# Attention scores of two query blocks written together, with their two causal masks as neighbours on TensorE

## Chip, core and metric

The kernel runs on one core of one Trainium2 chip. The metric is device time in microseconds, the median of several executions. One further execution is recorded by the hardware profiler; all rows below come from that one.

## The reference

A trunk of two layers for 1024 tokens of width 1024: a state-space layer, then keys, values and forget gates computed once, then an attention layer with 16 heads of 64. The change lies in the attention alone:

```python
s = jnp.einsum('bhqd,bhkd->bhqk', qi, kt)
s = s + fqi[..., None] - fk[:, :, None, :]
qpos = i * Q_BLOCK + jnp.arange(Q_BLOCK)
s = jnp.where(kpos[None, :] <= qpos[:, None], s, -jnp.inf)
p = jax.nn.softmax(s, axis=-1)
return jnp.einsum('bhqk,bhkd->bhqd', p, vt)
```

A block is 128 queries; block i sees the keys 0 to 128 (i + 1). Everything is float32.

## The kernel before

The state-space layer, the output of that layer and the tokens' keys, values and queries come first and fill the first 820 us. Float32 matmuls are split into parts that are exact in the chip's 4-byte matmul format, so that a product is two or three matmuls into one PSUM buffer.

The attention runs over 64 steps, `steps`: for each of 16 heads the four pairs of query blocks c = 0 to 3 (blocks 2c and 2c + 1, so 128 and 256 keys for c = 0, up to 896 and 1024 keys for c = 3). The loop at L1140 does `ahead` for the step two further on, which calls `scores`, then `values` for the present step, then some matmuls of another product as filling (`zb`, the gate projection, later `f`, the output projection).

`scores(hd, c)` treats the two blocks of a step one after the other. Up to 512 keys are one piece, more are two. A piece is a PSUM buffer `sp`: two score matmuls (L1010, L1011; high and low part of the keys), and for a block's last piece a third one (L1013) with bf16 operands, the identity times a triangle of 1e30 that hides the later keys. One VectorE instruction (L1015) adds the forget term, writes the piece to `pr` and leaves the running minimum in `mx` (the signs are turned round). Then come Exp on ScalarE (L1018), a reciprocal on VectorE (L1019) and the scaling on GpSimd (L1020).

`values` transposes the scaled rows on TensorE (`tp`, L1043), copies them rounded on ScalarE (`pth`, L1045), takes what rounding lost on VectorE (`ptl`, L1046), multiplies both with the values (`ov`, L1049 and L1050) and adds the two halves of the result (`oc`, L1056, after the copy `ob`, L1052). The gate's strips end with L991 on ScalarE and L992 on VectorE.

What is shared: `sp` has three PSUM buffers (pool `psb`), `tp` three (`psa`), `ov`, `zb` and `f` two together (`pj`); `pr` has two SBUF buffers for each c. The order of the instructions on each engine is not the order of the text: a list scheduler, which works with times of its own, lays it down when the kernel is built, and each engine then runs its list in order. `tc.issue_after(x)` keeps what it encloses behind `x` on x's engine.

Of the kernel before, what the change touches and what calls it, by code (L numbers as in the profile page):

```python
# [12 lines left out]
F32 = mybir.dt.float32  # L13
F32R = mybir.dt.float32r
BF16 = mybir.dt.bfloat16
AF = mybir.ActivationFunctionType
ALU = mybir.AluOpType
# [3 lines left out]
P = 128  # L21
# [25 lines left out]
def trunk(tc, a, out):  # L47
    nc = tc.nc
    V, S, G, T, Q = nc.vector, nc.scalar, nc.gpsimd, nc.tensor, nc.sync
    top = ExitStack()  # L50
    with top:
# [24 lines left out]
        vec, at0 = {}, 0  # L76
# [105 lines left out]
        with l0:  # L182
# [89 lines left out]
            for k in range(KT):  # L272
# [3 lines left out]
                if k < 2:  # L276
                    w01[k] = weight_strip(a["a_w_in"][k], [P, KT, P])
                V.scalar_tensor_tensor(out=s_a[:, k:k + 1], in0=mod[:, 8 + k:9 + k], scalar=sc1[:, k:k + 1], in1=ga[:, k:k + 1],
                                       op0=ALU.add, op1=ALU.mult)
                for i in range(2):  # L280
                    hi, xs = act[0][k][i][:, 0:HL], xt[:, HL * i:HL * i + HL]
                    S.activation(hi, xs, AF.Copy, scale=s_a[:, k:k + 1])
                    V.scalar_tensor_tensor(out=act[1][k][i][:, 0:HL], in0=xs, scalar=s_a[:, k:k + 1], in1=hi.bitcast(F32),
                                           op0=ALU.mult, op1=ALU.subtract)
# [12 lines left out]
            for k in range(KT):  # L297
                last_mod = mod_tile(k)
                hi, b = act[0][k][1][:, HL:], vec["modb"][:, k:k + 1]
                m = mod[:, k:k + 1].broadcast_to([P, 2])  # L300
                S.activation(hi, m, AF.Identity, bias=b)
                last_lo = V.scalar_tensor_tensor(out=act[1][k][1][:, HL:], in0=m, scalar=b, in1=hi.bitcast(F32),
                                                 op0=ALU.add, op1=ALU.subtract).ins
# [407 lines left out]
            for k in range(KT):  # L711
                pool, tag = ((s5, "bb"), (s5, "bbs"), (s5, "x1m"), (s5, "x2m"), (sbm, "min_"), (s5, "ut"), (sb, "uu"), (sb, "uu"))[k]
# [21 lines left out]
        with l0b:  # L734
# [38 lines left out]
            for e, i in OUT_SEQ:  # L773
# [8 lines left out]
                if sum(seen) and n < 40:  # L782
                    with tc.issue_after(xd):
# [3 lines left out]
                                       op0=ALU.mult, op1=ALU.add)  # L787
# [26 lines left out]
        with l1a:  # L814
# [103 lines left out]
            for j, job in enumerate(("v0", "v2", "k0", "k2", "q0", "q2")):  # L918
                kind, n0 = job[0], int(job[1])
                if job == "q0":  # L920
# [11 lines left out]
                    at0 = top.enter_context(tc.tile_pool(name="at0", bufs=2, side="right", reuse_waits="tile"))  # L932
# [27 lines left out]
        at_ = top.enter_context(tc.tile_pool(name="at", bufs=2, reuse_waits="tile"))  # L960
        msk = at0.tile([P, P], BF16, name="msk", tag="msk", bufs=1)
        G.memset(msk, 0.0)
        G.affine_select(out=msk, in_=msk, compare_op=ALU.is_ge, fill=BIG, base=0, pattern=[[-1, P]], channel_multiplier=1)
        idb = at0.tile([P, P], BF16, name="idb", tag="idb", bufs=1)
# [29 lines left out]

        def scores(hd, c):
            kk, qs, vhl, fb = hd
            prs = []
            for qi in range(2):
                i = 2 * c + qi
                nk = P * (i + 1)  # L1000
                qsl = qs[:, P * i:P * i + P]
                pr = (at0 if c < 2 else at_).tile([P, 256 * c + 256], F32, name="pr", tag=f"pr{c}")
                mx = None
                cut = nk if nk <= 512 else max(nk - 512, 512) if nk != 640 else 384
                for lo, hi in ((0, cut), (cut, nk))[:2 if nk > 512 else 1]:
                    w_ = hi - lo
                    wm_ = max(w_, 256)
                    last = hi == nk
                    sp = psb.tile([P, 512], F32, name="sp", tag="psb")
                    T.matmul(sp[:, 0:wm_], qsl, kk[:, 0, lo:lo + wm_], start=True, stop=False)  # L1010
                    T.matmul(sp[:, 0:wm_], qsl, kk[:, 1, lo:lo + wm_], start=False, stop=not last)  # L1011
                    if last:
                        T.matmul(sp[:, w_ - P:w_], idb, msk, start=False, stop=True)  # L1013
                    m0, mx = mx, at0.tile([P, 1], F32, name="mx", tag="mx", bufs=8)
                    V.tensor_tensor_reduce(out=pr[:, lo:hi], in0=sp[:, 0:w_], in1=fb[:, lo:hi], scale=1.0,  # L1015
                                           scalar=3e38 if m0 is None else m0, op0=ALU.add, op1=ALU.min, accum_out=mx)
                sm = at0.tile([P, 1], F32, name="sm", tag="sm", bufs=8)
                S.activation(pr[:, 0:nk], pr[:, 0:nk], AF.Exp, scale=-1.0, bias=mx, accum_out=sm)  # L1018
                V.reciprocal(out=sm, in_=sm)  # L1019
                G.tensor_scalar(out=pr[:, 0:nk], in0=pr[:, 0:nk], scalar1=sm, scalar2=0.0,  # L1020
                                op0=ALU.mult, op1=ALU.add)
                prs.append(pr)
            return prs

        def values(n, hd, c, prs):
# [39 lines left out]
        def ahead(j):  # L1065
            n, c = steps[j]
            for m in (n, n + 1):
                if m < NH and m not in hds:
                    hds[m] = head(m)
            return scores(hds[n], c)  # L1070
# [146 lines left out]
```

## Time and profile before

| | |
|---|---|
| median of 3 runs (lowest, highest) | 1225.78 us (1220.67, 1227.47) |
| the profiled execution: its time, its span | 1223.69 us, 1221.9 us |
| TensorE, weight loads, VectorE, ScalarE, GpSimd busy | 95%, 83%, 69%, 50%, 30% of the span |
| first and last causal mask | 820.7 us, 1121.5 us |
| masks, score matmuls, reductions | 128, 384, 192 |

The span is the time from the first to the last instruction of the profiled execution. A matmul's row gives a start and a length that includes its way through the array, so neighbours overlap; what one costs is read from the distance between the ends (start plus length) of two neighbours. A figure in brackets at a row's end is idle time of the engine before it, with what ended it. "PE" is TensorE, "PEld" its loading of weights, "DVE" VectorE, "ACT" ScalarE, "POOL" GpSimd.

### The profile page before, as it was taken

To read this page: it belongs to the slowest core of one execution; us is meant where nothing else is said; L and a number is where in the kernel's file an instruction comes from. 1 tells how busy PE (TensorE), PEld (TensorE's weight loads), DVE (VectorE), ACT (ScalarE), POOL (GpSimd) and SP (SyncE) were. 2 spreads that over 40 slices of the span, in tenths; PEclk is the share of its full clock that TensorE was granted. 3 is DMA by queue.
4 is the path that set the end of the run, shared out by engine and by line. 5 is a ranking of instruction groups with operands and counts; after the bars stand their busy time and mean duration, and the time that the engine had idled before them with its cause. 6 is when DMAs were issued, how large, how long until landed. Compare 5 with 4: busy or idle time off the path is not lost.

```text
span 1221.9 us, 20599 instructions
## 1 busy us (share of the span) xinstructions
PE 1162.0 (95%) x7542; PEld 1017.3 (83%) x7542; DVE 848.9 (69%) x1724; ACT 605.1 (50%) x1138; POOL 367.8 (30%) x568
## 2 busy tenths in 40 slices
PE   8989898997899998899989999999999999999898
PEld 6778887887778876799989989998888888888686
DVE  7889899874498767746444664448787778887421
ACT  6565766665335324322213452227677777886310
POOL 4000000000000033600133463447576666764100
PEclk9999999998989999999999999999999999999999
DMA  9754666584974885247543277518796968871242
GB/s 352 220 173 117 171 169 164 154 233 126 334 249 129 281 312 167 90 154 233 200 148 139 83 214 152 156 70 182 132 188 124 171 122 155 156 138 27 94 165 78
DMA packets 113333, 205.30 MB, mean 168 GB/s; under 512 B 17072, under 2 KB 58160, under 8 KB 111696
## 3 DMA queue, kind: packets, MB, share of 16 engines
q1 hardware_dynamic: 86272, 161.44, 41.4%
q0 software_dynamic: 24960, 37.75, 18.1%
q10 hardware_dynamic: 2000, 4.79, 1.7%
q8 instruction: 60, 0.98, 0.3%
q14 instruction: 41, 0.34, 0.1%
HBM read 146.47 MB, written 46.20 MB: 158 GB/s over the span
## 4 chain that ended last, share of the span: by engine, by line
PE 57%; DVE 16%; DMA 12%; ACT 5%; issue 5%; SPq 2%; POOL 2%; ACTq 0%; POOLq 0%; DVEq 0%
PE tkps L851 16%; PE zb L112 7%; PE pj_f L112 5%; PE tp L1043 5%; DMA modw<-modw 4%; PE u L264 4%; PE ov L1049 3%; PE ov L1050 3%; PE sp L1010 3%; DMA v_d<-vt 3%; PE sp L1011 3%; PE pj_g L112 2%; DMA mwx<-modw 2%; PE f L112 2%; DVE w_lo L101 1%
## 5 line engine op out<-in xcount | busy, mean ns | idle before, releaser
L851 PE MATMUL tkps<-wvh,aH 128*128 128x256 f32 (+1 forms) x768 | 220.5, 287 | 7.3 <-DVE vt L863 4.0
L851 PE MATMUL tkps<-wvh,aL 128*128 128x256 f32 (+1 forms) x768 | 217.1, 283 | 1.4 <-DVE aL L167 1.4
L851 PE MATMUL tkps<-wvl,aH 128*128 128x256 f32 (+1 forms) x768 | 216.7, 282 | 0.0
L851 PEld LDWEIGHTS tkps<-wvh,aH 128*128 128x128 f32 x768 | 145.2, 189 | 9.8 <-DVE vt L863 4.9
L851 PEld LDWEIGHTS tkps<-wvh,aL 128*128 128x128 f32 x768 | 145.1, 189 | 2.1 <-DVE aL L167 1.8
L851 PEld LDWEIGHTS tkps<-wvl,aH 128*128 128x128 f32 x768 | 145.3, 189 | 0.3 <-issue 0.2
L1045 ACT ACTIVATE pth<-tp 128x512 fp32r<-128x512 f32 (+1 forms) x192 | 87.2, 489 | 61.4 <-PE ov L1049 34.7
L1018 ACT ACTIVATE pr<-pr,mx 128x128 f32<-128x128 f32 (+7 forms) x128 | 98.9, 773 | 22.4 <-DVE mx L1015 21.8
L1020 POOL TENSOR_SCALAR pr<-pr,sm 128x128 f32<-128x128 f32 (+7 forms) x128 | 96.2, 761 | 40.6 <-DVE sm L1019 40.5
L1046 DVE TENSOR_TENSOR ptl<-tp,pth 128x512 fp32r<-128x512 f32 (+1 forms) x192 | 101.3, 551 | 9.0 <-ACT pth L1045 8.6
L93 ACT ACTIVATE w_hi<-w_raw 128x1024 fp32r<-128x1024 f32 x49 | 51.6, 1053 | 86.4 <-PE pj_f L112 29.5
L1015 DVE CUSTOM_DVE_ANT_0 pr<-sp,fb 128x512 f32<-128x512 f32 (+3 forms) x128 | 72.8, 569 | 21.3 <-PE tp L1043 19.9
L1049 PE MATMUL ov<-pth,vhl 128*128 128x256 f32 x320 | 85.6, 299 | 0.1
L1043 PE MATMUL tp<-ident,pr 128*128 128x128 f32 x576 | 82.9, 273 | 0.0
L874 ACT ACTIVATE hsq<-tkps 128x256 f32<-128x256 f32 x64 | 24.6, 384 | 117.8 <-PE tkps L851 112.5
L132 DVE CUSTOM_DVE_ANT_0 modw<-modw,c_b 128x1024 f32<-128x1024 f32 x48 | 58.6, 1223 | 34.0 <-DMA modw<-modw 33.7
L1050 PE MATMUL ov<-ptl,vhl 128*128 128x256 f32 x320 | 81.0, 286 | 0.2 <-DVE ptl L1046 0.2
L1010 PE MATMUL sp<-kk,qs 128*128 128x256 f32 (+2 forms) x192 | 74.5, 388 | 2.2 <-DVE mx L1015 1.9
L1043 PEld LDWEIGHTS tp<-ident,pr 128*128 128x128 f32 x576 | 65.3, 140 | 7.1 <-POOL pr L1020 0.5
L794 POOL TENSOR_TENSOR sq<-sq,sq 128x512 f32<-128x512 f32 x12 | 19.0, 1585 | 173.3 <-ACT sq L790 173.3
L877 POOL TENSOR_TENSOR hms<-hms,nhalf 128x4 f32<-128x4 f32 x64 | 67.6, 1057 | 5.0
L876 POOL TENSOR_SCALAR hms<-hms 128x4 f32<-128x4 f32 x64 | 15.2, 237 | 176.3 <-DVE hms L875 172.4
(325 smaller groups left out, 3305.4 us busy)
## 6 DMA issues: line engine op xcount, KB each, us to landing
modw<-modw SPq DMA_DIRECT2D x48, 512.0 KB, 5.1
kk<-k_d POOLq DMA_DIRECT2D x32, 512.0 KB, 6.8
wvr<-kvq_w SPq DMA_DIRECT2D x12, 1024.0 KB, 5.5
mwx<-modw SPq DMA_DIRECT2D x16, 512.0 KB, 7.5
w_raw<-a_w_in SPq DMA_DIRECT2D x16, 512.0 KB, 5.2
v_d<-vt SPq DMA_DIRECT2D x32, 256.0 KB, 2.5
fb<-f_d SPq DMA_DIRECT2D x16, 512.0 KB, 8.9
vhl<-v_d POOLq DMA_DIRECT2D x16, 512.0 KB, 9.7
```

The costliest lines, as they stand in the source:

```text
L112: T.matmul(ps, w[wt][:, k, :], act[at][k][half], start=(k == k0 and n == 0), stop=(k == k1 and n == 2))
L851: T.matmul(ps[:, 0:nv], at, wt[:, k, 0:nv], start=(n == 0), stop=(n == 3 * KT - 1))
L877: G.tensor_tensor(out=ms, in0=ms, in1=nhalf, op=ALU.pow)
L1010: T.matmul(sp[:, 0:wm_], qsl, kk[:, 0, lo:lo + wm_], start=True, stop=False)
L1015: V.tensor_tensor_reduce(out=pr[:, lo:hi], in0=sp[:, 0:w_], in1=fb[:, lo:hi], scale=1.0, scalar=3e38 if m0 is None else m0, op0=ALU.add, o ...
L1018: S.activation(pr[:, 0:nk], pr[:, 0:nk], AF.Exp, scale=-1.0, bias=mx, accum_out=sm)
L1020: G.tensor_scalar(out=pr[:, 0:nk], in0=pr[:, 0:nk], scalar1=sm, scalar2=0.0, op0=ALU.mult, op1=ALU.add)
L1043: T.transpose(out=tp[:, b, :], in_=prs[qi][:, P * (b0 + b):P * (b0 + b) + P], identity=ident)
L1045: S.activation(pth[:, 0:m, dst], tp[:, 0:m, :], AF.Copy)
L1046: V.tensor_tensor(out=ptl[:, 0:m, dst], in0=tp[:, 0:m, :], in1=pth[:, 0:m, dst].bitcast(F32), op=ALU.subtract)
L1049: T.matmul(ov, vhl[:, b, :], pth[:, b - b0, :], start=(b == 0), stop=False)
L1050: end = T.matmul(ov, vhl[:, b, :], ptl[:, b - b0, :], start=False, stop=(b == nb - 1)).ins
```

## The change

`scores` now runs over the pieces and not over the blocks: first the first pieces of both blocks where there are two, with their reductions, then the last pieces of both, four score matmuls, then the two masks directly one behind the other, then the two reductions. The mask of the second block is held behind the mask of the first, and that one behind the last score matmul, by `issue_after`. Exp, reciprocal and scaling of both blocks follow. Both `pr` buffers of a step are taken at its beginning. The instructions are the same in number and shape.

```diff
-            for qi in range(2):
-                i = 2 * c + qi
-                nk = P * (i + 1)
...
-                for lo, hi in ((0, cut), (cut, nk))[:2 if nk > 512 else 1]:
...
-                    sp = psb.tile([P, 512], F32, name="sp", tag="psb")
-                    T.matmul(sp[:, 0:wm_], qsl, kk[:, 0, lo:lo + wm_], start=True, stop=False)
-                    T.matmul(sp[:, 0:wm_], qsl, kk[:, 1, lo:lo + wm_], start=False, stop=not last)
-                    if last:
-                        T.matmul(sp[:, w_ - P:w_], idb, msk, start=False, stop=True)
-                    m0, mx = mx, at0.tile([P, 1], F32, name="mx", tag="mx", bufs=8)
...
+            for last in (False, True):
+                for qi in range(2):
+                    nk, cut = cut_of(qi)
+                    lo, hi = (cut if nk > 512 else 0, nk) if last else (0, cut if nk > 512 else 0)
+                    if hi == lo:
+                        continue
...
+                    sp = psb.tile([P, 512], F32, name="sp", tag="psb")
                     T.matmul(sp[:, 0:wm_], qsl, kk[:, 0, lo:lo + wm_], start=True, stop=False)
+                    m = T.matmul(sp[:, 0:wm_], qsl, kk[:, 1, lo:lo + wm_], start=False, stop=not last).ins
+                    work.append((qi, lo, hi, sp))
+                if last:
+
+                    for qi, lo, hi, sp in work:
+                        with tc.issue_after(m):
+                            m = T.matmul(sp[:, hi - lo - P:hi - lo], idb, msk, start=False, stop=True).ins
+                for qi, lo, hi, sp in work:
+                    pr = prs[qi]
+                    m0, mxs[qi] = mxs[qi], at0.tile([P, 1], F32, name="mx", tag="mx", bufs=8)
+                    V.tensor_tensor_reduce(out=pr[:, lo:hi], in0=sp[:, 0:hi - lo], in1=fb[:, lo:hi], scale=1.0,
+                                           scalar=3e38 if m0 is None else m0, op0=ALU.add, op1=ALU.min, accum_out=mxs[qi])
```

With other rows to place, the scheduler lays down another order from the first scores on. In TensorE's list before, 61 masks stand ahead of a transpose and 67 ahead of another matmul; in the list after, the 64 pairs stand 21 times ahead of a transpose and 43 times ahead of another matmul. One place recurs in every second head: the step with 384 and 512 keys (c = 1) of an even head. On TensorE before, from the three transposes behind a strip of the gate projection on:

```order
L1043 MATMUL tp<-ident,pr 128x128 x3
L1010 MATMUL sp<-kk,qs 128x384
L1011 MATMUL sp<-kk,qs 128x384
L1013 LDWEIGHTS idb
L1013 MATMUL sp<-msk,idb 128x128
L1010 MATMUL sp<-kk,qs 128x512
L1011 MATMUL sp<-kk,qs 128x512
L1013 LDWEIGHTS idb
L1013 MATMUL sp<-msk,idb 128x128
L1043 MATMUL tp<-ident,pr 128x128 x4
```

The same place on TensorE after:

```order
L1053 MATMUL tp<-ident,pr 128x128 x3
L1012 MATMUL sp<-kk,qs 128x384
L1013 MATMUL sp<-kk,qs 128x384
L1053 MATMUL tp<-ident,pr 128x128 x8
L1012 MATMUL sp<-kk,qs 128x512
L1013 MATMUL sp<-kk,qs 128x512
L1019 LDWEIGHTS idb
L1019 MATMUL sp<-msk,idb 128x128
L1019 LDWEIGHTS idb
L1019 MATMUL sp<-msk,idb 128x128
```

Eight transposes moved ahead of the second block's matmuls, and the first block's mask moved behind them.

On VectorE the reductions of these two blocks (384 and 512 keys), the gate, and the subtractions for the next value matmuls stand in this order before (the buffers' numbers tell the rows apart):

```order
L1015 ISA pr_10135,mx_10140<-sp_10136,fb_9759 128x384
L1015 ISA mx_10140 128x1
L1015 ISA pr_10146,mx_10151<-sp_10147,fb_9759 128x512
L1015 ISA mx_10151 128x1
L992 SCALAR_TENSOR_TENSOR o_t3_8253<-o_t3_8253,zb3_1_9677 128x512
L1046 TENSOR_TENSOR ptl_10018<-tp_10021,pth_10017 128x3x128
L1019 RECIPROCAL sm_10142<-sm_10142 128x1
L1046 TENSOR_TENSOR ptl_10018<-tp_10027,pth_10017 128x4x128
L1019 RECIPROCAL sm_10153<-sm_10153 128x1
L1046 TENSOR_TENSOR ptl_10086<-tp_10087,pth_10085 128x4x128
L1056 TENSOR_TENSOR oc_9673<-ov_9948,ob_9966 64x256
```

And after:

```order
L1023 ISA pr_10135,mx_10145<-sp_10137,fb_9759 128x384
L1023 ISA mx_10145 128x1
L1023 ISA pr_10136,mx_10147<-sp_10140,fb_9759 128x512
L1023 ISA mx_10147 128x1
L992 SCALAR_TENSOR_TENSOR o_t3_8253<-o_t3_8253,zb3_1_9677 128x512
L1056 TENSOR_TENSOR ptl_10018<-tp_10021,pth_10017 128x3x128
L1056 TENSOR_TENSOR ptl_10018<-tp_10027,pth_10017 128x4x128
L1030 RECIPROCAL sm_10149<-sm_10149 128x1
L1056 TENSOR_TENSOR ptl_10086<-tp_10087,pth_10085 128x4x128
L1066 TENSOR_TENSOR oc_9673<-ov_9948,ob_9966 64x256
```

VectorE's list hardly moved there: one reciprocal went behind the sum of the halves. What moved is the mask that its first row waits for.

## Rows read from the trace of the kernel before

**Rows 1.** The page's busy line; busy time, clock, DMA of one stretch.

```profile
PE 1162.0 (95%) x7542; PEld 1017.3 (83%) x7542; DVE 848.9 (69%) x1724; ACT 605.1 (50%) x1138; POOL 367.8 (30%) x568
...
820.00:1127.00 307.00, 304.50 (x2027) 260.20 (x2027) 250.65 (x785) 225.46 (x532) 196.09 (x342) 1.00 0.74 139
```

**Rows 2.** Who waited for whom: us in total, times, longest; TensorE, 820 to 1130.

```profile
PE sp L1010 <- DVE mx L1015: 1.9, 5, 0.7
```

**Rows 3.** The masks' line: weight loads and idle time before them (us, times).

```profile
L1013 PEld LDWEIGHTS <-idb x128: 95/96/98, 820.7 to 1121.5; 128*128 128x128 bf16 x128
...
  issue: 13.7, 64
```

**Rows 4.** Timeline of TensorE around two masks: start, length, instruction.

```profile
903.29 0.39 PE L1011 MATMUL sp<-kk,qs 128*128 128x512 f32 x1
903.52 0.23 PE L1013 MATMUL sp<-msk,idb 128*128 128x128 bf16 x1
903.56 0.36 PE L1010 MATMUL sp<-kk,qs 128*128 128x256 f32 x1
903.76 0.28 PE L1011 MATMUL sp<-kk,qs 128*128 128x256 f32 x1
903.88 0.23 PE L1013 MATMUL sp<-msk,idb 128*128 128x128 bf16 x1
903.94 0.94 PE L1043 MATMUL tp<-ident,pr 128*128 128x128 f32 x7
```

**Rows 5.** The weight loads at the first of these masks.

```profile
903.06 0.19 PEld L1011 LDWEIGHTS sp<-kk,qs 128*128 128x128 f32 x1
903.51 0.10 PEld L1013 LDWEIGHTS <-idb 128*128 128x128 bf16 x1 [0.26 <-issue]
```

**Rows 6.** TensorE at the recurring place, 927.8 to 934.3.

```profile
927.80 0.49 PE L1043 MATMUL tp<-ident,pr 128*128 128x128 f32 x3
...
928.30 0.33 PE L1011 MATMUL sp<-kk,qs 128*128 128x384 f32 x1
928.48 0.23 PE L1013 MATMUL sp<-msk,idb 128*128 128x128 bf16 x1
...
933.07 0.93 PE L1043 MATMUL tp<-ident,pr 128*128 128x128 f32 x7
934.01 0.39 PE L1049 MATMUL ov<-pth,vhl 128*128 128x256 f32 x1
```

**Rows 7.** VectorE at the same place, and two rows shortly before.

```profile
924.63 0.69 DVE L1046 TENSOR_TENSOR ptl<-tp,pth 128x512 fp32r<-128x512 f32 x1
925.24 0.74 DVE L1015 CUSTOM_DVE_ANT_0 pr<-sp,fb,mx 128x512 f32<-128x512 f32 x1
...
928.75 0.56 DVE L1015 CUSTOM_DVE_ANT_0 pr<-sp,fb 128x384 f32<-128x384 f32 x1
...
929.78 0.69 DVE L1015 CUSTOM_DVE_ANT_0 pr<-sp,fb 128x512 f32<-128x512 f32 x1 [0.47 <-PE tp L1043]
...
930.40 0.68 DVE L992 SCALAR_TENSOR_TENSOR o_t<-o_t,zb 128x512 f32<-128x512 f32 x1
931.00 0.55 DVE L1046 TENSOR_TENSOR ptl<-tp,pth 128x384 fp32r<-128x384 f32 x1
931.47 0.15 DVE L1019 RECIPROCAL sm<-sm 128x1 f32<-128x1 f32 x1
...
932.80 0.69 DVE L1046 TENSOR_TENSOR ptl<-tp,pth 128x512 fp32r<-128x512 f32 x1 [0.33 <-ACT pth L1045]
933.53 0.43 DVE L1056 TENSOR_TENSOR oc<-ov,ob 64x256 f32<-64x256 f32 x1
```

**Rows 8.** Who waited for the sum of the halves (us, times), 820 to 1127.

```profile
  PEld ov L1049: 1.8, 7
```

**Rows 9.** What ended TensorE's idle time before scores; one such wait.

```profile
  DVE mx L1015: 4.3, 10
...
1064.46 0.41 PE L1010 MATMUL sp<-kk,qs 128*128 128x384 f32 x1 [0.68 <-DVE mx L1015]
```

More of the change, by code (lines that the diff above doesn't have):

```diff
@@ L996, in scores, with cut_of @@
             kk, qs, vhl, fb = hd
-            prs = []
-            for qi in range(2):
-                i = 2 * c + qi
-                nk = P * (i + 1)
[L1001 to L1004, printed above, removed]
-                for lo, hi in ((0, cut), (cut, nk))[:2 if nk > 512 else 1]:
-                    w_ = hi - lo
-                    wm_ = max(w_, 256)
-                    last = hi == nk
+            def cut_of(qi):
+                nk = P * (2 * c + qi + 1)
+                return nk, nk if nk <= 512 else max(nk - 512, 512) if nk != 640 else 384
@@ new lines, in scores @@
+            prs = [(at0 if c < 2 else at_).tile([P, 256 * c + 256], F32, name="pr", tag=f"pr{c}") for _ in range(2)]
+            mxs, work = [None] * 2, []
+            for last in (False, True):
[4 more added lines that the diff above has]
+                        continue
+                    wm_ = max(hi - lo, 256)
+                    qsl = qs[:, P * (2 * c + qi):P * (2 * c + qi) + P]
@@ L1009, in scores @@
                     sp = psb.tile([P, 512], F32, name="sp", tag="psb")
                     T.matmul(sp[:, 0:wm_], qsl, kk[:, 0, lo:lo + wm_], start=True, stop=False)
-                    T.matmul(sp[:, 0:wm_], qsl, kk[:, 1, lo:lo + wm_], start=False, stop=not last)
-                    if last:
-                        T.matmul(sp[:, w_ - P:w_], idb, msk, start=False, stop=True)
-                    m0, mx = mx, at0.tile([P, 1], F32, name="mx", tag="mx", bufs=8)
-                    V.tensor_tensor_reduce(out=pr[:, lo:hi], in0=sp[:, 0:w_], in1=fb[:, lo:hi], scale=1.0,
-                                           scalar=3e38 if m0 is None else m0, op0=ALU.add, op1=ALU.min, accum_out=mx)
+                    m = T.matmul(sp[:, 0:wm_], qsl, kk[:, 1, lo:lo + wm_], start=False, stop=not last).ins
@@ L1017, in scores @@
+                work = []
+            for qi in range(2):
+                pr, nk = prs[qi], P * (2 * c + qi + 1)
                 sm = at0.tile([P, 1], F32, name="sm", tag="sm", bufs=8)
-                S.activation(pr[:, 0:nk], pr[:, 0:nk], AF.Exp, scale=-1.0, bias=mx, accum_out=sm)
+                S.activation(pr[:, 0:nk], pr[:, 0:nk], AF.Exp, scale=-1.0, bias=mxs[qi], accum_out=sm)
                 V.reciprocal(out=sm, in_=sm)
@@ L1021, in scores @@
                                 op0=ALU.mult, op1=ALU.add)
-                prs.append(pr)
             return prs
```

## The prediction

> **What bounds the kernel now.** I read the page's busy line first, then the table by stretches, then who waits for whom in the attention stretch, and only then single instructions. The change touches nothing before 820 us and nothing after the last causal mask at 1121.5 us, so the stretch 820 to 1127 us is all that can move. In it TensorE has an instruction under way for 304.5 of 307 us at a granted clock of 1.00, VectorE for 250.7 and ScalarE for 225.5 [rows 1]. TensorE's waits that the profile names for its matmuls of the scores are 1.9 us in five places [rows 2]. So TensorE sets the pace, and the other engines decide only at a few places where their chains are late. The sum below is therefore a sum over TensorE's stream, and after it comes a look at those places.
>
> **What a mask costs.** The 128 mask matmuls are the only ones with bf16 operands; all their neighbours are 4-byte. The unit that loads weights stood idle for 13.7 us in 64 places just before the masks' loads and was waiting for nothing that the profile shows [rows 3]. One of these: the weights of the last score matmul were loaded from 903.06, and the mask's load begins only at 903.51, when that matmul's columns have gone through, although the unit was free for 0.26 us [rows 5]. So a mask's load is not drawn ahead over its 4-byte neighbour. The price is read from ends of matmuls [rows 4]. The score matmul before the mask ends at 903.29 + 0.39 = 903.68 and the mask at 903.52 + 0.23 = 903.75: the mask costs 0.07 us itself. The matmul behind it, 256 columns wide, ends at 903.92, 0.17 after the mask, whereas the next of the same width takes 0.12 (904.04). So 0.05 us more is lost on the way out. Where transposes follow, nothing is lost on the way out: the mask at 903.88 ends at 904.11, the seven transposes at 904.88, which is 0.11 each, their usual spacing.
>
> **The change, part by part.** No instruction is added or taken away: 384 score matmuls, 128 masks, 192 reductions, the same Exp, reciprocals and scalings.
>
> (1) *Neighbours.* In TensorE's order before, 61 of 128 masks are followed by a transpose and 67 by a matmul that pays the way out. In the order after, all masks stand in 64 pairs; a pair is followed 21 times by a transpose and 43 times by a matmul that pays. So the scheduler had already covered 61 ways out with transposes, and what goes is not 64 of them but 67 - 43 = 24. At 0.05 us each that is 1.2 us less.
>
> (2) *The second mask of a pair.* No row shows a mask behind a mask. I take 0.07 us, the price of a first mask, because its own 128 columns and load are the same; then this part is zero. The lower end is 0.04 us, the shortest step from a mask's start to the next matmul's start (903.52 to 903.56) [rows 4]: 64 x 0.03 = 1.9 us less. The upper end is a mask with a full way out, 0.12 us: 64 x 0.05 = 3.2 us more. Both ends stay for the range. The Trainium skill, "TensorE: Matmul & The Clock Gate", section "Back-to-back issue gap", gives about 81 ns per matmul for a sustained run of loads and matmuls of 128 columns; worked out from that figure, an estimate, a second mask would cost 0.01 us more than I take, 0.7 us over 64 pairs, which speaks against the change. No row here shows it, and the 0.07 us of the first mask lies below it.
>
> (3) *Reductions come later, at a place where VectorE is the late one.* A pair's two masks now follow both blocks' pieces, so the first block's reduction begins later. In most places nobody cares: the transposes of a block follow its mask by 11 us and more of TensorE's stream in both orders, apart from the first seven steps. It matters once in every two heads, where the step with 384 and 512 keys meets a strip of the gate projection (or, in the last, of the output projection). Before: three transposes begin at 927.80, the first block's matmuls end at 928.63 and its mask at 928.71 [rows 6]; VectorE starts that reduction at 928.75, and between its operations up to 933.5 it idles 0.47 and 0.33 us [rows 7]. The chain ends with the sum of the two halves of the output, 933.53 + 0.43 = 933.96, which frees a PSUM buffer, and TensorE's next value matmul starts at 934.01, late: its transposes had begun at 933.07 [rows 6]. Seven such waits make 1.8 us [rows 8]. After: from 927.80 TensorE has three transposes (to 928.29), the 384-wide pair of matmuls (0.34), eight transposes (8 x 0.11), the 512-wide pair (2 x 0.23), and then the mask (0.07), which ends at 930.04; the reduction starts at 930.08. Behind it VectorE now works without a break: 0.56 and 0.62 for the two reductions, 0.60 for the gate, 0.47 and 0.61 for two subtractions, 0.15 for a reciprocal, 0.73 for the third subtraction and what lies behind it [rows 7], together 3.74. The sum of the halves starts at 933.82 and not at 933.53, and TensorE goes on 0.3 us later. ScalarE, which had the Exp of the second block ahead of the third subtraction's input, now has it behind, so it is not the later one. This sequence stands at six places in the order after: 6 x 0.3 = 1.8 us more. The ends are 0 (if the gate's operation finds its input later and slips behind) and 0.6 us per place (if ScalarE is late by one more Exp), 0 to 3.6 us.
>
> (4) *Three score buffers, two of them held.* Pieces of scores share three PSUM buffers. A pair now holds two until both masks are done. TensorE's waits for a buffer, 4.3 us in ten places with those that other instructions end, lie in the first ten microseconds and around 1063 us, where VectorE also splits the gated outputs (0.68 us at 1064.46) [rows 9]. At the beginning the new order asks for a buffer after 0.5 to 1.2 us of TensorE's stream where it was 0.9 to 1.5, while a reduction of 384 keys keeps VectorE 0.56 us and the next one behind it 0.62 [rows 7]; around 1063 us a 384-wide second piece is reduced later than before, with two splits behind it. I put down 0.8 us more for both together, half of one reduction in three places; the ends are 0 and 2 us.
>
> **The sum**: -1.2 + 0 + 1.8 + 0.8 = +1.4 us. The profiled execution took 1223.69 us (span 1221.9), which would become 1225.1; it lies 2.1 us below the median of the runs, 1225.78, and on that the sum gives 1227.2. The three runs lie 6.8 us apart, so neither is the better base, and I take the middle, **1226.2 us**. The ends add up to -1.2 - 1.9 = -3.1 (1222.7) and -1.2 + 3.2 + 3.6 + 2.0 = +7.6 (1233.4). About 0.5%, 6.1 us, is what a measurement of this kernel can tell from no change.
>
> **Rivals.**
> *The masks flow.* The second mask costs 0.04 us and VectorE's chain gives nothing back: -1.2 - 1.9 = -3.1, 1222.7 us. For it: weights and operands of both masks have one type. Against it: VectorE has no idle time left in the chain of part 3, and even this is below what can be told from no change.
> *The buffers run out, slower.* With two of three buffers held, the ring becomes the limit in the steady part too. Counting TensorE's stream between the last matmul into a buffer and its next use at the spacings of the rows, the order before has 7 places under 1.5 us, all in the first 14 us, and the order after has 23, many of them in every second head. If VectorE is behind at the 16 new ones so that the reduction ends half a microsecond after the buffer is wanted, that is 8 us: 1225.8 - 1.2 + 8 = 1232.6 us. It decides from the point where a reduction ends later than 1.0 us behind its mask at the places with 0.95 us. For it: reductions of 0.56 and 0.62 us follow each other there. Against it: the first of the two needs 0.04 + 0.56 us behind its mask when VectorE is free [rows 6, 7], which is inside 0.95. The Trainium skill, "Trainium Kernel Development and Optimization", section "Best Practices", says that consistent bubbles can mean that PSUM ran out; in this trace the bubbles are 1.9 us by name [rows 2], so it does not yet hold here.
> *The pairs don't do what they say.* The second mask's weights wait for the first as after any change of type, and a mask costs 0.12 us in a pair too: -1.2 + 3.2 + 1.8 + 0.8 = +4.6, 1230.4 us.
>
> **How the numbers follow.** Forecast 0.65, the masks flow 0.13, the buffers run out 0.14, pairs that don't pay 0.08. Only the buffers' case reaches past +0.5% (1231.9), with a small part of the last: slower 0.14. Past -0.5% (1219.7) there is no case, only a sum of luck: faster 0.04. Same 0.82. The range takes in the first, second and fourth case, 1222 to 1231; the buffers' case is left out.
>
> **What would show it.** Right: pairs whose second mask starts about 0.07 us behind the first with a matmul ending 0.17 behind it; TensorE's value matmul at the six places late by 0.5 to 0.6 us in all, freed by the sum of the halves; score matmuls waiting for the reductions' maximum 5 to 6 us in all. Part 2 is wrong if the second mask takes 0.04 or 0.12. Part 3 is wrong if VectorE's chain there has gaps or ScalarE ends it. The whole is wrong if score matmuls wait for the maximum in every second head, or if the stretch from the first mask to the last moves by over 6 us.

## The result and the profile after

The changed kernel took 1230.53 us (median of 14 runs, 1226.2 to 1235.21) and the kernel before 1224.51 (14 runs beside them, 1220.67 to 1229.13). The ratio is 1.0048, 95% interval 1.0033 to 1.0064: about 6 us slower, just inside half a per cent. In a second series it was 1228.12 us against 1224.08, ratio 1.0034 (1.0018 to 1.0049).

The page's busy line of the changed kernel, and its table by stretches (length; busy time of TensorE, its weight loads, VectorE, ScalarE, GpSimd with counts; granted clock; DMA share; GB/s). 824.61 us is the end of the last token matmul, the last work ahead of attention:

```profile
PE 1166.3 (95%) x7542; PEld 1026.5 (83%) x7542; DVE 845.2 (69%) x1724; ACT 603.2 (49%) x1138; POOL 367.4 (30%) x568
...
824.61:829.61 5.00, 1.68 (x13) 1.16 (x10) 2.21 (x5) 1.65 (x3) 1.20 (x2) 1.00 0.07 27
829.61:834.61 5.00, 4.97 (x25) 3.97 (x24) 3.60 (x17) 2.83 (x10) 2.23 (x8) 0.66 0.85 288
834.61:1131.00 296.39, 293.79 (x1963) 255.62 (x1963) 237.93 (x756) 216.39 (x514) 191.60 (x330) 1.00 0.75 138
```

The same two stretches of the kernel before, from the end of its last token matmul at 820.22:

```profile
820.22:825.22 5.00, 3.88 (x25) 2.50 (x23) 3.57 (x13) 3.29 (x9) 2.06 (x4) 1.00 0.05 21
825.22:830.22 5.00, 4.89 (x29) 3.62 (x29) 4.85 (x19) 3.95 (x11) 2.40 (x7) 1.00 0.84 295
```

The loss is to be seen in the first rows. In the first five microseconds of attention TensorE was busy for 3.88 before and is busy for 1.68 now; in the next five it is busy all the time, but at a granted clock of 0.66. In the long rest it is as full as in [rows 1].

TensorE's waits between the last token matmul and the last mask, by what ended them (us, times, longest; of waits over 0.15 us); they answer [rows 2], where five waits for the maximum made 1.9 us:

```profile
PE trps L886 <- DVE hnt L879: 1.9, 1, 1.9
PE sp L1012 <- DVE kl L891: 1.5, 1, 1.5
PE sp L1012 <- DVE mx L1023: 1.3, 1, 1.3
PE ov L1060 <- DVE ptl L1056: 0.5, 1, 0.5
```

**A measure that the experiments share.** Ten of the thirteen traces of this study have the same instructions up to the last token matmul, and it ended anywhere from 816.5 to 824.6 us. In six of them (both of the changed kernel, not the one before) a stretch of 3.4 us between 771 and 782 us had half the clock, after waits that the others have too. This scatter is no part of the change, and 1.6 us of the 9.3 us by which the first two spans differ are that stretch. So the traces are compared over **the stretch from the end of the last token matmul to the end of the last mask**: 301.46 us before (820.22 to 1121.69), 306.37 in the changed kernel (824.61 to 1130.98), 306.36 in its second trace.

Where the +4.91 us lie is worked out matmul by matmul: the distance from the end of one to the end of the next, less the median distance for its width in the kernel before. For the masks the whole distance stands. A "way out" is what the matmul behind a mask loses; the first two rows together are called mask terms below.

| us, in the stretch | before | after | difference |
|---|---|---|---|
| masks themselves (128; after: 64 first, 64 second) | 9.3 | 8.1 | -1.2 |
| ways out behind masks | 3.7 | 1.6 | -2.1 |
| waits in the first ten microseconds | 3.1 | 4.1 | +1.0 |
| matmuls at half clock there, beyond normal | 0 | 1.9 | +1.9 |
| value matmuls behind a pair, eleven places of 0.18 | 0 | 2.0 | +2.0 |
| six places with 384 and 512 keys | 1.8 | 3.0 | +1.2 |
| steps right after the beginning, to 865 us | 0.3 | 0.9 | +0.6 |
| around 1063 us, and 1083 to 1115 | 2.9 | 3.5 | +0.6 |
| all other matmuls, some 1,750 | 0.2 | 0.8 | +0.7 |

The rounded rows add up to 4.7 of the 4.91 us. So the neighbours did what the change is named for (-1.2 and -2.1), and the loss lies mainly in three other places: the beginning, the value matmuls behind a pair, and the six places with 384 and 512 keys. The experiments took them one by one.

### The profile page after: what moved, and what is told of

The parts are those of the page before. It is cut to its first block, busy times and chain, and to the rows that moved or that the text cites. A ratio compares the mean times of both kernels' runs of the same rounds, so it can differ in the third digit from the quotient of the medians.

```text
span 1231.2 us, 20643 instructions
## 1 busy us (share of the span) xinstructions
PE 1166.3 (95%) x7542; PEld 1026.5 (83%) x7542; DVE 845.2 (69%) x1724; ACT 603.2 (49%) x1138; POOL 367.4 (30%) x568
## 5 line engine op out<-in xcount | busy, mean ns | idle before, releaser
L1056 DVE TENSOR_TENSOR ptl<-tp,pth 128x512 fp32r<-128x512 f32 (+1 forms) x192 | 98.6, 549 | 13.2 <-ACT pth L1055 12.6
L1023 DVE CUSTOM_DVE_ANT_0 pr<-sp,fb 128x512 f32<-128x512 f32 (+3 forms) x128 | 70.0, 569 | 22.9 <-PE tp L1053 14.3
L1053 PE MATMUL tp<-ident,pr 128*128 128x128 f32 x576 | 78.9, 273 | 0.0
```

Of the source, the lines that this page charges most:

```text
L1023: V.tensor_tensor_reduce(out=pr[:, lo:hi], in0=sp[:, 0:hi - lo], in1=fb[:, lo:hi], scale=1.0, scalar=3e38 if m0 is None else m0, op0=ALU.a ...
L1053: T.transpose(out=tp[:, b, :], in_=prs[qi][:, P * (b0 + b):P * (b0 + b) + P], identity=ident)
L1056: V.tensor_tensor(out=ptl[:, 0:m, dst], in0=tp[:, 0:m, :], in1=pth[:, 0:m, dst].bitcast(F32), op=ALU.subtract)
```

## The three places in the trace

**The entry.** TensorE from the last token matmuls to the first pair (start, length, instruction; in brackets the idle time and what ended it):

```profile
824.45 0.38 PE L886 MATMUL trps<-ident,hnt 128*128 128x128 f32 x2
824.59 0.37 PE L1012 MATMUL sp<-kk,qs 128*128 128x256 f32 x1
824.79 0.38 PE L886 MATMUL trps<-ident,hnt 128*128 128x128 f32 x2
824.93 0.36 PE L1013 MATMUL sp<-kk,qs 128*128 128x256 f32 x1
825.13 0.38 PE L886 MATMUL trps<-ident,hnt 128*128 128x128 f32 x2
827.38 0.44 PE L886 MATMUL trps<-ident,hnt 128*128 128x128 f32 x2 [1.86 <-DVE hnt L879]
829.27 0.39 PE L1012 MATMUL sp<-kk,qs 128*128 128x256 f32 x1 [1.45 <-DVE kl L891]
829.49 0.28 PE L1013 MATMUL sp<-kk,qs 128*128 128x256 f32 x1
829.62 0.29 PE L1019 MATMUL sp<-msk,idb 128*128 128x128 bf16 x2
829.93 0.69 PE L1012 MATMUL sp<-kk,qs 128*128 128x384 f32 x1
830.41 0.52 PE L1013 MATMUL sp<-kk,qs 128*128 128x384 f32 x1
```

The masks and the last of these transposes in the kernel before, whose last token matmul ends at 820.22:

```profile
820.74 0.23 PE L1013 MATMUL sp<-msk,idb 128*128 128x128 bf16 x1
...
821.71 0.23 PE L1013 MATMUL sp<-msk,idb 128*128 128x128 bf16 x1
...
822.93 0.23 PE L1013 MATMUL sp<-msk,idb 128*128 128x128 bf16 x1
...
823.11 0.38 PE L886 MATMUL trps<-ident,hnt 128*128 128x128 f32 x2
```

The last transposes of the queries (`trps`) write into the same pool of three PSUM buffers (`psb`) as the scores, and two of their tiles are still being filled: their last input, `hnt` (normalised queries, from VectorE), comes 2.7 us behind the last token matmul. In the kernel before this wait was filled: the first block's piece was masked, reduced and its buffer taken again, so that three masks and six score matmuls ran ahead of the last `trps`, which ended 3.3 us behind the last token matmul there and 3.2 us in the changed kernel. In the changed kernel the first piece holds the third buffer until the second is there too, and the second needs a buffer of the transposes, which comes free only with `kl` (what rounding the transposed queries lost, taken by VectorE), shortly ahead of 829.27. The first block's mask, whose matmuls end at 825.29, stands behind it. Then the clock falls: from 829.96 to 833.37 the granted clock is 0.5, and the 384-wide matmul at 830.41 takes 0.52 us, 0.33 in [rows 6]. (The one at 829.93 also holds a short wait and the way out behind the masks.)

**A value matmul behind a pair.** TensorE, and VectorE at the same time:

```profile
893.62 0.28 PE L1013 MATMUL sp<-kk,qs 128*128 128x256 f32 x1
893.74 0.28 PE L1019 MATMUL sp<-msk,idb 128*128 128x128 bf16 x2
893.93 0.39 PE L1060 MATMUL ov<-ptl,vhl 128*128 128x256 f32 x1
```

```profile
892.04 0.69 DVE L1023 CUSTOM_DVE_ANT_0 pr<-sp,fb 128x512 f32<-128x512 f32 x1 [1.08 <-PE tp L1053]
...
892.65 0.61 DVE L1023 CUSTOM_DVE_ANT_0 pr<-sp,fb,mx 128x384 f32<-128x384 f32 x1
...
893.19 0.68 DVE L1056 TENSOR_TENSOR ptl<-tp,pth 128x512 fp32r<-128x512 f32 x1
```

The two masks end 0.12 us behind the score matmul (893.90 to 894.02), but the value matmul ends at 894.32, 0.30 behind the masks, where the exit from a mask to a value matmul took 0.17 before (a mask from 886.32 for 0.23 us, the value matmul behind it from 886.36 for 0.36). It reads `ptl`, which VectorE has ready at 893.87. VectorE had waited 1.08 us with the second block's unmasked reduction (892.04) at the head of its queue, for transposes of an earlier step; the first block's masked reduction was queued behind that one and the subtraction `ptl` behind both. In the kernel before, `ptl` stood between two reductions of one block [rows 7: 924.63, then 925.24].

**The place with 384 and 512 keys**, the counterpart of [rows 6] and [rows 7], in another head (TensorE, then VectorE):

```profile
899.54 0.39 PE L1013 MATMUL sp<-kk,qs 128*128 128x512 f32 x1
899.81 0.38 PE L1012 MATMUL sp<-kk,qs 128*128 128x256 f32 x1
900.03 0.28 PE L1013 MATMUL sp<-kk,qs 128*128 128x256 f32 x1
900.41 0.50 PE L112 MATMUL zb<-aH,w_hi 128*128 128x512 f32 x1
...
901.91 0.93 PE L1053 MATMUL tp<-ident,pr 128*128 128x128 f32 x7
902.59 0.38 PE L1059 MATMUL ov<-pth,vhl 128*128 128x256 f32 x1
```

```profile
898.58 0.56 DVE L1023 CUSTOM_DVE_ANT_0 pr<-sp,fb 128x384 f32<-128x384 f32 x1 [1.20 <-PE sp L1019]
...
899.06 0.69 DVE L1023 CUSTOM_DVE_ANT_0 pr<-sp,fb 128x512 f32<-128x512 f32 x1
...
899.67 0.68 DVE L992 SCALAR_TENSOR_TENSOR o_t<-o_t,zb 128x512 f32<-128x512 f32 x1
...
902.11 0.43 DVE L1066 TENSOR_TENSOR oc<-ov,ob 64x256 f32<-64x256 f32 x1
```

VectorE's reductions are late and without a break between them, as forecast, but the operation that TensorE waits for is the gate (`o_t`, over at 900.35), which frees the PSUM buffer that the next strip's matmul at 900.41 takes: 0.36 us lost there, and 0.14 at the score matmul of 899.81, which needs a score buffer. The sum of the halves (`oc`) ends at 902.54 and the value matmul at 902.59 is on time now. So 0.50 us are lost at the place where the kernel before lost 0.29, measured by the same distances, at its value matmul (the waits of [rows 8]).

## Experiments

All ratios are to the kernel before, run beside each kernel. "Stretch" is the one defined above (301.46 before, 306.37 after). `scores_old` is the function of the kernel before, put beside the new one.

**The changed kernel again.**

> The changed kernel once more, unaltered, to have a second trace of it. In the first pair of traces TensorE's stream of the changed kernel was already 4.4 us late at the last transposes ahead of attention, where both programs have the same instructions. Theory A (the loss lies in the attention: the first pair finds too few score buffers, and one place in every two heads is 0.25 us longer) expects a ratio to the kernel before of about 1.004, a first mask that starts about 3 us later behind the last of those transposes than in the kernel before, and any lead of the part ahead of attention to vary from trace to trace. Theory B (every pair of masks costs) expects the same 1.004, but no such delay at the entry. Theory C (the 6 us are scatter of the part ahead of attention) expects a ratio within 1.002.

Ratio 1.0034 (1.0018 to 1.0049), stretch 306.36, first mask 5.1 us behind the last token matmul (0.5 before). The loss is in the attention and repeats; theory C, scatter, is out for it. The delay is 4.6 us where 3 were expected.

**The first two steps as before.**

```diff
-            return scores(hds[n], c)
+            return (scores_old if j < 2 else scores)(hds[n], c)
```

> The changed kernel, with the scores of the first two steps (two of 64) written as before: each block's pieces, its mask and its reduction in one go. Theory A: TensorE no longer stands still for 1.9 and 1.5 us in front of the first scores, no half-clock stretch follows, and the time falls by about 3 us from the changed kernel's, to a ratio of about 1.002 to the kernel before. Theory B: two of 64 pairs are nothing, at most 0.2 us less than the changed kernel, ratio 1.0045. Theory C: no difference from the changed kernel or the kernel before, all within 1.002.

Ratio 1.0007 (0.9987 to 1.0026), stretch 303.60. Two of 64 pairs cost 2.8 us of the stretch and 3.3 us of the time (1.0034 to 1.0007). First mask 0.5 us behind the last token matmul; no half clock in the stretch.

**The new order of pieces without neighbours.**

```diff
-                    m = T.matmul(sp[:, 0:wm_], qsl, kk[:, 1, lo:lo + wm_], start=False, stop=not last).ins
+                    T.matmul(sp[:, 0:wm_], qsl, kk[:, 1, lo:lo + wm_], start=False, stop=not last)
...
-                if last:
-
-                    for qi, lo, hi, sp in work:
-                        with tc.issue_after(m):
-                            m = T.matmul(sp[:, hi - lo - P:hi - lo], idb, msk, start=False, stop=True).ins
+                    if last:
+                        T.matmul(sp[:, hi - lo - P:hi - lo], idb, msk, start=False, stop=True)
```

> The changed kernel's order of pieces (first both blocks' unmasked pieces, then both masked ones, then the reductions), but each mask directly behind its own score matmuls, with no wait for the other block's. It tells the new order of the pieces from the neighbours. Theory A: the second piece does not hold the first one's mask back, so the entry is like the kernel before's; the masks pay their way out alone again (about 24 x 0.05 us = 1.2 us more than neighbours), and the place in every two heads is early again: ratio about 1.000 to 1.001. Theory B: also 1.000, since no mask has a neighbour. Rival D (the order of the pieces and of the reductions itself is what costs): ratio 1.004 as for the changed kernel.

Ratio 1.0017 (0.9998 to 1.0036), stretch 304.49, first mask on time. Both lie between theory A (1.000 to 1.001) and rival D (1.004): the stretch is 3.0 us longer than before, 0.25% of the time, with no neighbours and no delay at the entry. Rival D is right in part: the order of pieces and reductions costs by itself. The value matmuls behind a mask end 0.25 us after it at ten places here too (0.17 before).

**The first two steps and the place with 384 and 512 keys of every even head as before.**

```diff
-            return scores(hds[n], c)
+            return (scores_old if j < 2 or (c == 1 and n % 2 == 0) else scores)(hds[n], c)
```

> The changed kernel, with the scores written as before in the first two steps and in the step with 384 and 512 keys of every even head (the place where VectorE's chain frees TensorE's PSUM buffer late). Some 55 of 64 pairs stay neighbours. Theory A: both sources of the loss are gone, and what stays are second masks at 0.056 us and fewer ways out: 0.5 to 1.5 us below the kernel before, ratio 0.999 to 1.000, and some 1.5 us below the kernel with only the first two steps as before. Theory B: 55 of 64 pairs still cost, ratio 1.0038. Theory C: within 1.002, like all the others.

Ratio 0.9986 (0.9970 to 1.0003), stretch 302.13: 1.5 us below the kernel with only the first two steps as before, as expected, 0.24 us for each of six places. But the stretch is still 0.7 us longer than before's, where pairs alone should have made it shorter; the eleven places of 0.30 us are all there. The ratio alone says 1.7 us less than before, and the two don't agree: its interval ends at +0.4 us.

**All pairs kept, the last transposes of the queries in another pool.**

```diff
-                    tr = psb.tile([P, 4, P], F32, name="trps", tag="psb")
+                    pool, tag = (psa, "psa") if dst is q_d and pr0 == 6 and i == 1 else (psb, "psb")
+                    tr = pool.tile([P, 4, P], F32, name="trps", tag=tag)
```

> The changed kernel, all 64 pairs kept; only the last two groups of the queries' transposes (trps, the second half of the last strip) write into the pool of three PSUM buffers that the token tiles and the transposes of the scores use (psa), and not into the one that the scores use (psb). It tests the cause of the delay at the entry by itself. Buffer theory: the first pair finds its second buffer free, so the first mask starts about 0.6 to 1 us behind the last token matmul and not 5.0 us, the waits of 1.9 us for hnt and 1.5 us for kl ahead of the first scores are gone, no half-clock stretch follows, and the time falls by about 3 us from the changed kernel's, to a ratio to the kernel before of about 1.001, as for the kernel with its first two steps as before (1.0007). Rival: what delays the entry is the hold itself (a first mask that waits for a second score), then the waits stay and the ratio is 1.0035 as for the changed kernel (1.0034 on this chip).

Ratio 1.0019 (0.9998 to 1.0041), stretch 304.98. TensorE at the entry (the last token matmul ends at 816.46):

```profile
816.53 0.28 PE L1014 MATMUL sp<-kk,qs 128*128 128x256 f32 x1
816.65 0.38 PE L887 MATMUL trps<-ident,hnt 128*128 128x128 f32 x2
816.87 0.27 PE L1020 MATMUL sp<-msk,idb 128*128 128x128 bf16 x2
816.95 0.42 PE L1013 MATMUL sp<-kk,qs 128*128 128x384 f32 x1
...
822.18 0.41 PE L1054 MATMUL tp<-ident,pr 128*128 128x128 f32 x2 [1.44 <-POOL pth L1048]
```

The first mask comes 0.4 us behind the last token matmul with its pair held as in the changed kernel: the hold alone doesn't delay the entry, it does so where the transposes have the buffers. The gain is only half of what was expected (1.4 us of the stretch for about 3), since a new wait of 1.44 us stands at 822 us and a half-clock stretch follows that one (824.5 to 827.4 at 0.51 in the table by stretches), 1.8 us beyond normal.

**The other pool, and the place with 384 and 512 keys as before.** The diffs of the pool and of `scores_old if c == 1 and n % 2 == 0`.

> As the kernel before this one, and also the step with 384 and 512 keys of every even head with its scores as before (56 of 64 pairs stay). If entry and that place add up, each with its own cause, it is 1.0 to 1.5 us below the kernel with only the buffers moved, and within 1 us of the kernel that had the first two steps and that place as before (ratio 0.9986): expected 0.998 to 1.000. If the six places only hide a wait that comes back later, there is no difference between the two.

Ratio 1.0005 (0.9983 to 1.0026), a little above what was expected and unclear by itself. The stretch is 301.28, 3.7 us below the one with only the pool: 1.8 of it is the half-clock stretch, which is not there (the wait ahead of it is); 1.9 are left, where 1.0 to 1.5 was expected of the six places. So far as these two traces tell, the two causes add up.

**The steps with 896 and 1024 keys as before, too.** `scores_old if j < 2 or c == 3 or (c == 1 and n % 2 == 0)`.

> The kernel with the first two steps and the 384/512 place of every even head as before (ratio 0.9986), and in addition all steps with 896 and 1024 keys as before; 39 of 64 pairs stay. In the traces of every kernel with pairs there, the value matmul behind a pair of masks ends 0.30 us after the mask and not 0.17, at 10 to 12 places, since VectorE has two reductions of that step in a row ahead of the subtraction (ptl) that the matmul reads. Theory E (VectorE's order is what costs there): these waits go, 10 x 0.125 = 1.2 us less, and 16 pairs that are taken apart cost 16 x (0.016 + about 0.03) = 0.7 us more: the attention stretch in the trace gets 0.5 us shorter, which a ratio can hardly tell (0.998 to 0.999). Rival: a value matmul behind a pair costs 0.30 us whatever VectorE does (the switch from bf16 to 4-byte weights after two bf16 loads): the places behind the remaining pairs keep 0.30 us, and the stretch gets about 0.7 us longer.

Ratio 1.0016 (0.9991 to 1.0040), unclear; stretch 303.43. The places of 0.30 us are gone with VectorE's order: twelve value matmuls that stand behind a pair end 0.17 us after it, so the switch of types is not what cost there. Eleven of the twelve read `pth` and one `ptl`, while all eleven late ones of the changed kernel read `ptl`; the wait goes with `ptl`. Three more that read `ptl` end 0.36 to 1.03 us after their pairs, from 1063 us on; two of them wait 0.6 us for it. But the stretch got 1.3 us longer, not 0.5 shorter: mask terms are 12.0 us against 10.1, and two score matmuls that end at 835.4 and 837.3 us now wait for the reductions' maximum, 0.5 us in all. Taking the pairs apart is the wrong remedy.

**All pairs kept, the reductions block by block.** The second block's unmasked piece is reduced behind both pieces of the first.

```diff
-                for qi, lo, hi, sp in work:
+                late = work[1:] if not last else []
+                for qi, lo, hi, sp in (sorted(kept + work, key=lambda p: p[:2]) if last else work[:1]):
...
-                work = []
+                kept, work = late, []
```

> The changed kernel with the reductions written block by block: the first block's two, then the second block's two, where the changed kernel reduces both unmasked pieces first. All 64 pairs of masks stay neighbours. It tells the order of VectorE's reductions from the hold. If the order of the reductions is what delays the subtractions, the 0.30 us places go and the attention stretch is 1 to 1.5 us shorter than the changed kernel's; the entry is unchanged (3 to 4 us late), so the ratio is 1.002 to 1.003. If buffers are what counts, the second block's unmasked piece now keeps its buffer longer, score matmuls wait for it (up to 0.5 us at 32 places), and the ratio goes to 1.006 or more.

Ratio 0.9997 (0.9974 to 1.0020), stretch 300.82 with the entry still 4.7 us late and at half clock. That is 5.5 us shorter than the changed kernel's, where 1 to 1.5 was expected: the expectation was right in its direction and far too low. From the 129th matmul of the gate's strips (876.7 us in the kernel before) to the last mask it gains 3.1 us on the kernel before, where the changed kernel lost 1.8. The scheduler also orders TensorE anew with it: a pair is now followed by transposes 34 times, by value matmuls 20 times and by scores 9 times (21, 12 and 31 in the changed kernel). A pair with a value matmul behind it, and VectorE there:

```profile
887.25 0.29 PE L1019 MATMUL sp<-msk,idb 128*128 128x128 bf16 x2
887.35 0.36 PE L1060 MATMUL ov<-pth,vhl 128*128 128x256 f32 x1
```

```profile
887.23 0.69 DVE L1057 TENSOR_TENSOR ptl<-tp,pth 128x512 fp32r<-128x512 f32 x1 [0.28 <-ACT pth L1056]
887.84 0.61 DVE L1024 CUSTOM_DVE_ANT_0 pr<-sp,fb,mx 128x384 f32<-128x384 f32 x1
...
888.37 0.68 DVE L1024 CUSTOM_DVE_ANT_0 pr<-sp,fb 128x512 f32<-128x512 f32 x1
```

The subtraction now stands ahead of both reductions, and the value matmul ends 0.17 us behind the masks (887.54 to 887.71). This one reads `pth`; ten that read `ptl` behind a pair end 0.17 us after it in this kernel too, where eleven took 0.30. The 0.50 us at the places with 384 and 512 keys are down to 0.11 to 0.12 at five of the six; at the sixth, with the output projection, they stay 0.51.

**The reductions by block, and the first two steps as before.** The diffs of the two kernels.

> Pairs of masks with the reductions written block by block, and the first two steps' scores as before, so that the entry has no delay; 62 of 64 pairs stay neighbours. If the entry (3 to 4 us) and the order of VectorE's reductions (3.1 us in the steady part of the trace) were the changed kernel's two losses, the neighbours' own gain now shows: the attention stretch from the last token matmul to the last mask is 3 to 4 us shorter than the kernel before's, and the ratio is about 0.997. If instead the kernel with reductions by block only had luck (its stretch was 0.6 us shorter than before's although its entry was 4.7 us late), the ratio is 0.9995 to 1.001.

Ratio 0.9978 (0.9962 to 0.9995), 1221.34 us against 1223.30; stretch 299.20, 2.3 us shorter than before's and 7.2 shorter than the changed kernel's. This version is faster than the kernel before by 0.2%, which the interval just holds apart from nothing.

**The reductions by block, all pairs, and the other pool.** The diffs of the two kernels.

> All 64 pairs with the reductions written block by block, and the last two groups of the queries' transposes in the other pool, so that the first pair finds its buffers. Same theory: first mask 0.4 us behind the last token matmul, no 2 us wait for hnt ahead of it, stretch 2 to 4 us shorter than the kernel before's, ratio 0.997 to 0.999. In the one trace with the other pool and the changed kernel's order of reductions, a transpose waited 1.6 us for ScalarE at 820.7 and a half-clock stretch of 3.4 us followed; if that comes with the other pool, the ratio is 0.999 and the kernel with the first two steps as before is the better one.

Ratio 0.9985 (0.9966 to 1.0005), stretch 300.39. The wait of 1.4 us for `pth` and a half-clock stretch behind it (821.5 to 824.9, 2.0 us) came with the other pool, so by the stretch, 1.2 us longer, it is the weaker remedy, as the expectation said it would then be. The two ratios don't tell them apart.

**The reductions by block, no neighbours.** The edits of the kernel without neighbours and of the one by block.

> The same order of pieces and of reductions as the kernel with pairs and reductions by block, but each mask directly behind its own score matmuls: no mask has a neighbour, and the entry is as before. It prices the neighbours alone, against the kernel with 62 pairs, the same reductions and the same entry. From the traces of the pairs (second mask 0.056 us for 0.072, and 60 fewer ways out of 0.03 to 0.05 us) neighbours are worth about 3 us: expected ratio 1.000, with mask terms of 12 to 13 us in the trace against 9.5. If the neighbours are worth nothing and the order of the reductions is the whole gain, it has the ratio of the kernel with 62 pairs.

Ratio 1.0007 (0.9987 to 1.0027), stretch 302.22. The loader's idle time ahead of the masks' weights, of this kernel and then of the one with 62 pairs (its 124 masks in pairs):

```profile
  issue: 13.8, 64
```

```profile
  issue: 8.5, 31
```

Against the kernel with 62 pairs, mask terms are 13.2 us for 9.8, the stretch is 302.22 for 299.20, and the ratio is 1.0007 for 0.9978. Neighbours are worth 3.0 to 3.5 us by all three readings, once nothing else gives it back. The ratios alone tell less, since their intervals overlap (0.9987 to 1.0027 and 0.9962 to 0.9995).

## Why the prediction held, and where its sum failed

The forecast was 1226.2 us with a range of 1222 to 1231, "within half a per cent"; 1230.53 and 1228.12 lie in it, near its end. The direction was right. That the time lies in the range is in part luck: the sum of +1.4 us stands against +4.9 in the stretch and about 6 in the time, and the upper end of 1231 was there for pairs that don't pay, a case that did not come. The largest loss lay outside the forecast's own measure: it would have been given up if the stretch from the first mask to the last had moved by over 6 us, and that moved by 0.4 (300.9 to 301.4). The delay came ahead of the first mask.

- **Part 1, neighbours: right.** Forecast -1.2. Ways out fell from 3.7 to 1.6 us; with 0.05 us of ordinary way out for each of the eleven value matmuls that the table has in a row of their own, the part comes to -1.5. That the scheduler had covered most ways out by itself was read rightly.
- **Part 2, the second mask: wrong by size, on the good side.** I took a second mask for as dear as a first, 0.07. A first one costs 0.072, a second 0.056 from end to end, 64 x 0.016 = 1.0 us less. The end of 0.04 was not reached, and the estimate of 0.01 us more for a second mask did not come true either.
- **Part 3: right place and size, wrong link, and the list of places was short.** Six places at 0.22 make +1.2 (forecast 1.8), and they vanished when that step was written as before (-1.5). But the gate's buffer decides there, not the sum of the halves that the forecast named as its sign. The step that failed is "in most places nobody cares": it asked only how soon the block's own transposes follow its mask. What cares is what is queued behind the reductions on VectorE, and `ptl` there has a value matmul waiting: eleven places at 0.125 beyond the normal way out, 1.4 us.
- **Part 4: the step that failed most.** It had 0.8 us for the beginning and 1063 us together, at most 2. The entry alone cost 2.9 us, 1.0 in waits and 1.9 at half clock. It was right that two of three buffers are held, and it counted scores only. The last transposes of the queries hold two buffers of the same pool for 3 us; the diff doesn't show them, the tag `psb` of line 884 does. The half clock behind such a wait was not in the sum at all. The sign that the forecast named, score matmuls that wait 5 to 6 us in all for the maximum, did not come: the loads of their weights wait for it 3.1 us in seven places, fewer than the 4.3 in ten of [rows 9], and 3.3 us in three places for `kl`. Around 1063 us the term was right, nearly nothing.
- **The rivals.** "The masks flow" had the masks nearly right (-2.5 by parts 1 and 2, -3.1 forecast) and assumed that VectorE gives nothing back. "The buffers run out" had the right resource and the wrong place: score matmuls lost 0.14 us at six places of the steady part, not 0.5 at sixteen, and the buffers ran out for long only at the entry. "The pairs don't do what they say" is out.

That the order of the reductions loses about as much as the neighbours gain was in no case. It is shown by the kernels with reductions by block: reducing block by block takes 2.3 us off the stretch without neighbours (304.49 to 302.22) and 4.4 with 62 pairs (303.60 to 299.20). Open is the 0.7 us spread over all other matmuls (the other kernels with pairs have roughly 0.2 to 0.7 us more there than the kernel before, the two without about 0.25), and how much of the gain by block is VectorE's order and how much the new order on TensorE that comes with it.

## What to carry to other kernels

Before two results are made to wait for each other, list every user of the pool they lie in, also of the stage before, and look at the handover between stages first: there a held buffer stops an engine that has nothing else to do. When an engine's operations are put together for one consumer's sake, ask what stood between them in its queue and who waits for that. A gain of 3 us on TensorE, the engine that sets the pace, was real here and was given back at places that are no part of it.

## What the runs showed of the hardware that was not expected

- A mask of 128 bf16 columns right behind another ends 0.056 us after it, a first one 0.072 us after a 4-byte matmul. In a pair the loader of weights stood idle ahead of the first mask's load only: the profile lists 9.1 us in 32 places in the changed kernel, 13.7 in 64 in [rows 3]. The second load came at once: the two loads at 829.61 take 0.11 us together, one alone 0.10.
- Two waits of 1.86 and 1.45 us within four microseconds were followed by 3.4 us at half the clock (1.2 GHz), in both traces of the changed kernel and in the one with its late entry and the reductions by block. The price was 1.9 us in the first of them, where the waits had added 1.0. A wait of 1.4 us in the kernels with the other pool was followed by such a stretch in two of three traces.
- The same instructions ahead of attention ended up to 8.1 us apart in ten traces. One span of each kernel could not have told any of these terms.
